# One 128x128 score product per chunk in a gated linear attention layer, with the prompt's keys scaled by 2^-16

## The chip, the cores and the metric

The kernel runs on one core of a Trainium2 chip. The metric is the device time of one execution in microseconds (us). TensorE is called PE in the profile (its weight loads PEld), VectorE DVE, ScalarE ACT, GpSimd POOL, and SyncE, which issues most of the transfers, SP.

## The reference

One decoder layer for 1024 prompt tokens and 32 sample tokens (8 sequences of 4), 1024 wide. An input projection feeds two groups: a recurrent group of 4 heads (HGRN2, a gated linear attention) and a convolution group with 31 taps. An output projection merges them. What matters here is the recurrent group:

```python
q = silu(q)
f = lb + (1 - lb) * sigmoid(fp);  k = 1 - f;  logf = log(f)
# per head, S is 128x128:  S_t = diag(f_t) S_{t-1} + k_t v_t^T ,  o_t = S_t^T q_t
o_a = rmsnorm(o_a, a_norm_g) * silu(za)
```

## The kernel before

**Projection.** `project` computes one block of 128 output channels for all 1056 tokens (1024 + 32). The inputs are split into a high and a low part (`wh`, `wl` of the weights; two tiles named `big` of the activations), and 3 x 24 matmuls of 128x352 run into three of four PSUM banks named `mm`. There are 24 such projections in the order `gb0 ga0 gb1 ga1 f0 q0 f1 q1 gb2 ga2 f2 q2 gb3 ga3 f3 q3`, then `za0..3` and `zb0..3`. The first part of the kernel, up to some 111 us, also makes the values `vt`; the output projection fills the time from some 390 us to the end.

**Heads.** Beside the projections two lists of generators are pumped: `hq` with the heads (`hgrn`) and `bg` with the convolution (`conv`), whose 30-odd taps per channel block are DVE instructions of about 512 elements. A head takes the prompt in two halves of 512 tokens, each of four chunks of 128 tokens; so there are 4 heads x 2 halves = 8 score blocks. In a half of the guarded fast path:

- `base` makes `qb` = q exp(g - m) and `kb` = k exp(m - g) on DVE and ACT, g being the running sum of log f in a chunk and m its value at token 63 (tiles `hw`);
- PE turns `kb` (`aux<-ident,hw`), ACT copies the result to `kT` (tile `ho`);
- PE makes the scores of each chunk in the bank `ptps` (`ptps<-hw`): 64 early keys against all 128 queries, and 64 late keys against the 64 late queries, the second with `tile_position=(0, 64)`. The quarter that neither writes was set to zero once by a memset;
- DVE copies the scores under a causal mask to `pt` (`COPY_PREDICATED`);
- PE makes the four chunks' state increments (`aux<-vt,ho`), DVE adds them up in `st`;
- PE adds `ops<-hw,st` (old state) and `ops<-pt,vt` (scores times values), and `head_norm` normalises over the head with ACT's Ln and Exp.

A 128x128 product in plain f32 (scores, state increments, outputs) leaves two MATMUL records in the trace; the projections' split products leave one each.

**The guard.** The fast path holds if the decay within half a chunk stays in a range (`RANGE`); a flag, computed in the kernel, starts a second, slower version (`emit` with `fast=False`) where it does not. That version is not executed here.

**What sets the order.** The program is written in the order of `project` and the pumps. A scheduler then orders the instructions of each engine by a simulated time with priorities, so a change of one instruction's length can move others. Each engine executes its own list in order.

Of the kernel before, what the change touches and what calls it, by code (L numbers as in the profile page):

```python
# [32 lines left out]
EPS = 1e-6  # L33
LB_MIN = 0.02
RANGE = 60.0
VPOS = 4
LEAD = 10.0
HU = 3
# [58 lines left out]
def emit(nc, tc, h, fast, flag_out=None):  # L97
    HW = 5
    with ExitStack() as ctx:
# [25 lines left out]
        make_identity(nc, ident)  # L125
        eps = sb([P, 1], "eps")
        nc.vector.memset(eps, EPS)
        avgr = sb([P, P], "avg", dt=F32R)
        avg = avgr.bitcast(F32)
        av = sb([P, P], "st", 5)  # L130
# [225 lines left out]

        lb = sb([P, 4], "lb")
        omlb = sb([P, 4], "omlb")
        nomlb = sb([P, 4], "nomlb")
        l0 = cols[:, C_LOG : C_LOG + 4]  # L360
        l1 = cols[:, C_LOG + 4 : C_LOG + 8]
        lt = sb([P, 12], "lt")
# [5 lines left out]
        V.reciprocal(lt[:, 0:4], lt[:, 0:4])  # L368
        V.tensor_tensor(lb, lt[:, 4:8], lt[:, 0:4], ALU.mult)
        V.tensor_scalar(omlb, lb, -1.0, 1.0, ALU.mult, ALU.add)  # L370
        V.tensor_scalar(nomlb, lb, -1.0, None, ALU.add)
        if fast:
            rng = sb([P, H, 16], "rng")
        wsum = sb([P, 60], "wsum")
# [87 lines left out]
        def hgrn(hd, q, k, g):  # L462
# [15 lines left out]
            for hf in range(2):  # L478
# [29 lines left out]
                    V.tensor_tensor(d3[:, :, r], d3[:, :, r], q3[:, :, r], ALU.mult)  # L508
                    return d

                def base(blk, idx, src=gv, n=512, mk=hw, qq=qv, kk=kv):
                    d = rel(blk, idx, src, n, mk)
                    kb = mk()
                    S.activation(kb, d, AF.Exp, scale=-1.0)
                    S.activation(d, d, AF.Exp)
                    V.tensor_tensor(kb, kb, kk, ALU.mult)
                    V.tensor_tensor(d, d, qq, ALU.mult)
                    return d, kb

# [3 lines left out]
                if fast:  # L523
# [8 lines left out]
                    S.copy(kT, kps)  # L532
                    for c in range(4):
                        cs = slice(c * P, (c + 1) * P)
                        c1, ce = c * P + P // 2, c * P + P

                        T.matmul(
                            ptps[0:64, cs], lhsT=kb[:, c * P : c1], rhs=qb[:, cs],
                            start=True, stop=True,
                        )  # L540
                        T.matmul(
                            ptps[64:P, c1:ce], lhsT=kb[:, c1:ce], rhs=qb[:, c1:ce],
                            start=True, stop=True, tile_position=(0, 64),
                        )
                    for pr in range(2):
                        masked(
                            pts[pr],
# [116 lines left out]
                        stop=True,  # L664
                    )
                yield
                yield from head_norm(hd, c0, 512, ops)
            if fast:
                end = sb([P, P], "st", 5)
                V.tensor_scalar(end, st, eg[:, 8:9], None, ALU.mult)  # L670
                st = end
            nc.sync.dma_start(h["o_hp"][hd], st)
            yield
# [4 lines left out]
            def sm():  # L678
# [6 lines left out]
            ki = rel(NS, NS - 1, gv, ST, sm)  # L685
            S.activation(ki, ki, AF.Exp, scale=-1.0)
            k4 = sb([P, 4, ST], "kts", 3)
            V.tensor_tensor(
                k4,
                ki.unsqueeze(1).to_broadcast([P, 4, ST]),  # L690
                kv.unsqueeze(1).to_broadcast([P, 4, ST]),
                ALU.mult,
            )
            kps = aux()
# [29 lines left out]
            yield  # L724
            sps = aux()
            if fast:
                qb, kb = base(NS, 1, gv, ST, sm, qv, kv)
                pairs = [(kb, qb)]
            else:
                pairs = []  # L730
                for hs in LEVELS[-2:]:
                    a = level(hs, gv, ST, sm, qv, kv)
                    pairs.append((a, a))
                pairs.append((kv, qv))
# [49 lines left out]
                    )  # L784
            nc.sync.dma_start(h["o_hs"][hd], so)
            yield
            yield from head_norm(hd, SEQ, ST, ops)
            hdone.add(hd)

        def head_norm(hd, c0, n, ops):  # L790
            lo = sb([P, 512], "ho", 2, F32R)
            hi = sb([P, 512], "ho", 2, F32R)
            r = late["mixa"][:, hd, c0 : c0 + n]
            S.activation(hi[:, 0:n], ops[:, 0:n], AF.Square)
            S.activation(r, ops[:, 0:n], AF.Square)
            V.tensor_tensor(lo[:, 0:n], r, hi[:, 0:n].bitcast(F32), ALU.subtract)
            ms = aux()
            mean(ms[:, 0:n], hi[:, 0:n], lo[:, 0:n])
            S.activation(r, ms[:, 0:n], AF.Ln, bias=eps)  # L799
            S.activation(r, r, AF.Exp, scale=-0.5)  # L800
            V.scalar_tensor_tensor(
                r, ops[:, 0:n], cols[:, C_HG : C_HG + 1], r, ALU.mult, ALU.mult
            )
            yield

# [161 lines left out]
        for i, (kind, c) in enumerate(order):  # L967
            if i == VPOS:
                t0 = T.ns
                for tb in range(2, 8):  # L970
                    v_block(tb)
                T.ns = t0
                ptps = bank("ptps", 1)
                V.memset(ptps, 0.0)
                late["ptps"] = ptps
                mixa = late["mixa"] = big()
            if i + 1 < len(order):
                ws.append(load_w(base_of[order[i + 1][0]] + order[i + 1][1]))
            w = ws.pop(0)
            nd = 1  # L980
            if kind == "gb":
                u = sb([P, 4 * MB], "u", 2)
                nc.gpsimd.memset(u[:, 0:PAD], 0.0)
                nc.sync.dma_start(
                    u[:, UW:UEND].rearrange("p (b t) -> p b t", t=PAD + NS)[:, :, 0:PAD], h["sc"][c]
                )
                cur["u"] = u
                project(
                    w, glu_evac(u, AF.Sigmoid, cols[:, C_BGLU + 4 + c : C_BGLU + 5 + c]), nd
                )  # L990
            elif kind == "ga":
                u = cur["u"]
                project(w, glu_evac(u, None, cols[:, C_BGLU + c : C_BGLU + c + 1]), nd)
                nc.sync.dma_start(h["o_cp"][c], u[:, SEQ:UW])
                nc.sync.dma_start(
                    h["o_cs"][c],
                    u[:, UW:UEND].rearrange("p (b t) -> p b t", t=PAD + NS)[:, :, NS:],
                )
                bg.append(conv(c, u))
                if c == 3:  # L1000
                    def lnp():
                        ln_pre()
                        yield

                    bg.insert(len(bg) - 1, lnp())
                    bg.append(ln_main())
            elif kind == "f":
                kt = sb([P, TOK], "qkg", 5)
                g = sb([P, TOK], "qkg", 5)
                project(w, act_into(kt, AF.Sigmoid), nd)  # L1010
                S.activation(g, kt, AF.Ln, bias=lb[:, c : c + 1], scale=omlb[:, c : c + 1])
                S.activation(
                    kt, kt, AF.Identity, bias=omlb[:, c : c + 1], scale=nomlb[:, c : c + 1]
                )
                for hf in range(4):
                    gs = g[:, hf * 256 : hf * 256 + 256]
                    V.tensor_tensor_scan(gs, rst, gs, 0.0, ALU.mult, ALU.add)
                gs = g[:, SEQ:TOK]
                V.tensor_tensor_scan(gs, rsts, gs, 0.0, ALU.mult, ALU.add)
                cur["kt"], cur["g"] = kt, g  # L1020
            elif kind == "q":
                q = sb([P, TOK], "qkg", 5)
                project(w, act_into(q, AF.Silu), nd)
                hq.append(hgrn(c, q, cur["kt"], cur["g"]))
            elif kind == "za":
                z = silu_tile()
                project(w, act_into(z, AF.Silu), nd)
                while c not in hdone:
                    step(hq)
                V.tensor_tensor(mixa[:, c, :], mixa[:, c, :], z, ALU.mult)  # L1030
            else:
                z = silu_tile()
                zb.append(z)
                if c == 2:
                    while not ln_state["done"]:
                        step(bg)
                    n0 = len(ln_state["done"])
                    project(
                        w,
                        act_into(z, AF.Silu),  # L1040
                        nd,
                        more=[partial(ln_silu, j, nb) for nb in range(n0) for j in range(4)],
                    )
                    for nb in range(n0):
                        ln_gate(nb, range(3))
                elif c == 3:
                    drain(1000)
                    project(
                        w,
                        act_into(z, AF.Silu),  # L1050
                        0,
                        (0, 1, 2),
                        more=[partial(ln_silu, j, nb) for nb in range(n0, 3) for j in range(4)],
                    )
                    for nb in range(3):
                        ln_gate(nb, range(3, 4) if nb < n0 else range(4))
                else:
                    project(w, act_into(z, AF.Silu), nd)
            if kind == "ga" and c == 0:
                V.ns = T.ns  # L1060
# [295 lines left out]
```

## Time and profile before

| | |
|---|---|
| median of 3 runs | 500.35 us (499.99 to 501.29) |
| the profiled execution | 500.03 us, its span 498.2 us |
| busy PE, DVE, ACT | 484.2, 358.6, 250.6 us |
| granted TensorE clock | 0.993 |
| DMA | 43.52 MB, mean 87 GB/s |

The page lists busy time by engine, the span in 40 slices, the chain of work that ended last and the costliest groups of instructions. In a timeline a row reads: start, duration, engine, line, operation, output<-inputs, shape, count, and in brackets the idle time of the engine before it with what ended it. PE's matmuls are pipelined, so the records overlap; what a piece of work costs PE is the time from start to start. `L72` is the line of a helper that records every DVE and PE operation, so the tile names tell the instructions apart.

### The profile page before, as it was taken

Reading aid. Unit: us, or ns where it says so; the run is one execution under the profiler, and the core shown is the slowest. Engines: PE = TensorE matmul, PEld = TensorE weight load, DVE = VectorE, ACT = ScalarE, POOL = GpSimd, SP = SyncE. Lnnn points to the kernel's source line nnn. Section 1 sums busy time; section 2 is a strip of 40 time slices with the busy share of each in tenths; the row PEclk is TensorE's granted clock in tenths of the full one; section 3 lists DMA queues with packets and bytes.
Section 4 is the critical chain, followed back from the end, with each engine's and each line's share of the span. In section 5 each row is a group of like instructions: output and inputs, shape, how many; then the busy total and the mean of one; then the engine's idle time right before and its main releaser. Section 6 shows DMA issues by size and latency. Waiting matters only on the chain.

```text
span 498.2 us, 7600 instructions
## 1 busy us (share of the span) xinstructions
PE 484.2 (97%) x3020; PEld 442.7 (89%) x3020; DVE 358.6 (72%) x682; ACT 250.6 (50%) x439; POOL 3.0 (1%) x20
## 2 busy tenths in 40 slices
PE   6999999999999999999999999999999999999992
PEld 5788899999999998999999999999999977877781
DVE  4864213999999989998999988993677747543441
ACT  5764332413646554635536554545766985422321
POOL 1000000000000000000000000000000000000000
PEclk9999999999999999999999999999999999999997
DMA  7910501231111213211123101131115396432111
GB/s 272 314 43 13 170 25 30 42 62 36 42 44 43 52 49 61 88 43 43 48 55 128 27 27 49 42 128 44 47 43 180 89 415 202 153 114 86 42 53 49
DMA packets 23003, 43.52 MB, mean 87 GB/s; under 512 B 10640, under 2 KB 11920, under 8 KB 22960
## 3 DMA queue, kind: packets, MB, share of 16 engines
q1 hardware_dynamic: 21808, 40.86, 26.3%
q10 hardware_dynamic: 1152, 2.10, 1.1%
q8 instruction: 25, 0.41, 0.3%
q14 instruction: 18, 0.15, 0.1%
HBM read 35.72 MB, written 7.24 MB: 86 GB/s over the span
## 4 chain that ended last, share of the span: by engine, by line
PE 90%; ACT 4%; DMA 3%; DVE 2%; issue 1%; SPq 0%; DVEq 0%
PE mm L72 70%; PE ops L72 8%; PE ptps L72 6%; PE aux L72 5%; DMA u<-gin 1%; ACT big L954 1%; DMA raw<-wo 1%; DMA o_hs<-raw 1%; DVE raw L72 1%; ACT L455 1%; DVE qkg L72 0%; ACT big L1100 0%; DVE big L72 0%; ACT qkg L455 0%; DVE u L72 0%
## 5 line engine op out<-in xcount | busy, mean ns | idle before, releaser
L72 PE MATMUL mm<-big,wh 128*128 128x352 f32 (+1 forms) x1280 | 323.7, 332 | 0.0
L72 PEld LDWEIGHTS mm<-big,wh 128*128 128x128 f32 x1280 | 224.1, 188 | 8.1 <-issue 1.6
L72 PE MATMUL mm<-big,wl 128*128 128x352 f32 (+1 forms) x640 | 211.4, 331 | 0.0
L72 PEld LDWEIGHTS mm<-big,wl 128*128 128x128 f32 x640 | 120.5, 188 | 3.4 <-issue 0.4
L72 DVE TENSOR_TENSOR wl<-wraw,wh 128x1024 fp32r<-128x1024 f32 x24 | 29.3, 1222 | 25.9 <-ACT wh L390 25.8
L72 DVE SCALAR_TENSOR_TENSOR big<-u,wsum,big 128x511 f32<-128x511 f32 (+14 forms) x60 | 44.5, 741 | 0.6
L72 DVE SCALAR_TENSOR_TENSOR big<-u,cols,big 128x511 f32<-128x511 f32 (+14 forms) x60 | 44.0, 735 | 0.0
L72 DVE SCALAR_TENSOR_TENSOR cq<-u,cols,cq 128x511 f32<-128x511 f32 (+13 forms) x56 | 41.2, 735 | 0.0
L72 DVE TENSOR_TENSOR qkg<-mm,big 128x512 f32<-128x512 f32 x16 | 10.9, 690 | 35.7 <-PE mm L72 35.7
L390 ACT CAST wh<-wraw 128x1024 fp32r<-128x1024 f32 x24 | 25.1, 1047 | 17.2 <-issue 7.8
L72 PE MATMUL mm<-vt,wh 128*128 128x512 f32 x64 | 25.6, 402 | 0.4 <-ACT wh L1167 0.4
L395 ACT ACT_TABLE_LOAD x20 | 25.7, 1283 | 0.3
L455 ACT ACTIVATE qkg<-mm 128x352 f32<-128x352 f32 x48 | 19.4, 465 | 11.4 <-PE mm L72 11.3
L72 PE MATMUL mm<-vt,wl 128*128 128x512 f32 x64 | 24.8, 390 | 0.0
L1204 ACT ACTIVATE big<-qkg 128x512 f32<-128x512 f32 x16 | 10.0, 628 | 29.1 <-DVE qkg L72 29.1
L455 ACT ACT_TABLE_LOAD x16 | 20.5, 1283 | 1.3 <-PE mm L72 1.0
L72 PE MATMUL ops<-big 128*128 128x512 f32 x64 | 20.8, 403 | 0.2 <-ACT big L197 0.2
L72 PE MATMUL ptps<-big 128*128 128x512 f32 x64 | 19.9, 394 | 0.0
L1167 ACT CAST wh<-big 128x512 fp32r<-128x512 f32 x16 | 9.2, 617 | 19.1 <-PE mm L72 18.6
L72 PEld LDWEIGHTS mm<-vt,wh 128*128 128x128 f32 x64 | 12.0, 188 | 5.2 <-ACT wh L1167 1.7
L72 PE MATMUL mm<-hw,wh 128*128 128x512 f32 x40 | 15.7, 392 | 0.0
L799 ACT ACTIVATE big<-aux,eps 128x512 f32<-128x512 f32 (+1 forms) x12 | 6.7, 556 | 17.9 <-PE aux L72 17.5
(239 smaller groups left out, 634.7 us busy)
## 6 DMA issues: line engine op xcount, KB each, us to landing
wraw<-win SPq DMA_DIRECT2D x24, 512.0 KB, 3.6
wraw<-wo SPq DMA_DIRECT2D x12, 512.0 KB, 3.7
big<-xp SPq DMA_DIRECT2D x2, 2048.0 KB, 10.1
big<-xp SPq DMA_DIRECT2D x4, 512.0 KB, 10.7
raw<-sh SPq DMA_DIRECT2D x4, 512.0 KB, 3.5
o_hs<-raw SPq DMA_DIRECT2D x4, 512.0 KB, 3.0
raw<-wo SPq DMA_DIRECT2D x4, 512.0 KB, 5.2
o_yp<-qkg ACTq DMA_DIRECT2D x8, 256.0 KB, 2.9
```

Of the source, the lines that this page charges most:

```text
L72: return f(*a, **k)
L390: S.copy(hi, wr)
L395: after(S.preload_act_table_set("natural_log_exp_and_others"), prev)
L455: return [S.activation(dst[:, nb * MB : (nb + 1) * MB], ps, func, bias=bias)]
L799: S.activation(r, ms[:, 0:n], AF.Ln, bias=eps)
L954: return S.activation(cv[:, c, cs], cv[:, c, cs], AF.Silu, bias=cols[:, C_LNB + c : C_LNB + c + 1], scale=cols[:, C_LNG + c : C_LNG + c + 1],)
L1167: S.copy(hv, m[:, :, ts])
L1204: S.activation(xr[:, hs], y[:, hs], AF.Square, accum_out=sqs[:, half : half + 1])
```

## The change

The two products of a chunk become one product of 128 keys by 128 queries, which fills the whole bank, and the memset of the bank goes. The late keys against the early queries, which the mask drops, are now computed too; so that they stay finite the keys are scaled by `KS` = 2^-16: the ACT instruction that makes k from the sigmoid takes its factors from `kb0` and `kw` (in place of `omlb` and `nomlb`). The factor is taken out again in the head's norm (`scale` of the Ln, and `hgk` in place of the gain), at the end in the final state (a second factor in the `TENSOR_SCALAR`), and for the sample tokens in two products, which become `SCALAR_TENSOR_TENSOR`.

```diff
-        nomlb = sb([P, 4], "nomlb")
+        kc = sb([P, 9], "kc")
+        kb0, kw, hgk = kc[:, 0:4], kc[:, 4:8], kc[:, 8:9]
...
-        V.tensor_scalar(nomlb, lb, -1.0, None, ALU.add)
+        V.tensor_scalar(kb0, lb, -ks, ks, ALU.mult, ALU.add)
+        V.tensor_scalar(kw, lb, ks, -ks, ALU.mult, ALU.add)
+        V.tensor_scalar(hgk, cols[:, C_HG : C_HG + 1], 1.0 / ks, None, ALU.mult)
...
                     S.activation(kb, d, AF.Exp, scale=-1.0)
                     S.activation(d, d, AF.Exp)
-                    V.tensor_tensor(kb, kb, kk, ALU.mult)
+                    if ks == 1.0:
+                        V.tensor_tensor(kb, kb, kk, ALU.mult)
+                    else:
+                        V.scalar_tensor_tensor(kb, kb, 1.0 / ks, kk, ALU.mult, ALU.mult)
...
                     for c in range(4):
                         cs = slice(c * P, (c + 1) * P)
-                        c1, ce = c * P + P // 2, c * P + P
-                        T.matmul(
-                            ptps[0:64, cs], lhsT=kb[:, c * P : c1], rhs=qb[:, cs],
-                            start=True, stop=True,
-                        )
-                        T.matmul(
-                            ptps[64:P, c1:ce], lhsT=kb[:, c1:ce], rhs=qb[:, c1:ce],
-                            start=True, stop=True, tile_position=(0, 64),
-                        )
+                        T.matmul(ptps[:, cs], lhsT=kb[:, cs], rhs=qb[:, cs], start=True, stop=True)
...
-                V.tensor_scalar(end, st, eg[:, 8:9], None, ALU.mult)
+                V.tensor_scalar(end, st, eg[:, 8:9], 1.0 / ks, ALU.mult, ALU.mult)
...
-            S.activation(r, ms[:, 0:n], AF.Ln, bias=eps)
+            S.activation(r, ms[:, 0:n], AF.Ln, bias=eps, scale=1.0 / (ks * ks))
...
                 ptps = bank("ptps", 1)
-                V.memset(ptps, 0.0)
```

The line numbers shift by one to three. The scheduler's order changes as well; three places follow.

PE, second half of head 1 (around 207 us in the trace of before). Before, the score products are broken up by the state increments and one output product:

```order
L72 MATMUL mm<-big,wl 128x352
L72 MATMUL ptps<-hw 64x128
L72 MATMUL ptps<-hw 64x64
L72 MATMUL ptps<-hw 64x128
L72 MATMUL aux<-vt,ho 128x128 x4
L72 MATMUL ptps<-hw 64x64
L72 MATMUL ops<-pt_421,vt 128x128
L72 MATMUL ptps<-hw 64x128
L72 MATMUL ptps<-hw 64x64
L72 MATMUL ptps<-hw 64x128
L72 MATMUL ptps<-hw 64x64
```

The same place in the changed kernel:

```order
L73 MATMUL mm<-big,wh 128x352
L73 MATMUL ptps<-hw 128x128 x4
L73 MATMUL mm<-big,wh 128x352
L73 MATMUL mm<-big,wl 128x352
L73 MATMUL mm<-big,wh 128x352 x2
L73 MATMUL mm<-big,wl 128x352
L73 MATMUL mm<-big,wh 128x352 x2
L73 MATMUL mm<-big,wl 128x352
L73 MATMUL mm<-big,wh 128x352 x2
L73 MATMUL aux<-vt,ho 128x128 x4
```

The four products now stand together, and the state increments come ten projection matmuls later. Counted in projection matmuls, the block's first score stands at 825 of 1728; before it stood at 803.

PE, second half of head 3 (around 333 us), before:

```order
L72 MATMUL mm<-big,wh 128x352 x2
L72 MATMUL ptps<-hw 64x128
L72 MATMUL aux<-vt,ho 128x128 x4
L72 MATMUL ptps<-hw 64x64
L72 MATMUL ptps<-hw 64x128
L72 MATMUL ptps<-hw 64x64
L72 MATMUL ptps<-hw 64x128
L72 MATMUL ptps<-hw 64x64
L72 MATMUL ptps<-hw 64x128
L72 MATMUL ptps<-hw 64x64
L72 MATMUL ops<-pt_421,vt 128x128
L72 MATMUL mm<-big,wl 128x352
```

and in the changed kernel:

```order
L73 MATMUL mm<-big,wh 128x352
L73 MATMUL ptps<-hw 128x128
L73 MATMUL aux<-vt,ho 128x128 x4
L73 MATMUL ptps<-hw 128x128 x2
L73 MATMUL ops<-pt_421,vt 128x128
L73 MATMUL ptps<-hw 128x128
L73 MATMUL mm<-big,wh 128x352
```

Here the block stays broken up, but all products in it now have one shape. From projection matmul 1546 on PE's list has the same instructions at the same places as before.

DVE, first half of head 0 (around 149 us): the first state copy `st<-aux`, which waits for the state increments, before:

```order
L72 SCALAR_TENSOR_TENSOR big<-u,cols,big 128x497
L72 COPY st<-aux 128x128
L72 TENSOR_TENSOR wl<-wraw,wh 128x1024
L72 SCALAR_TENSOR_TENSOR big<-u,wsum,big 128x501
L72 TENSOR_TENSOR hw<-hw,qkg 128x512
L72 SCALAR_TENSOR_TENSOR cq<-u,cols,cq 128x500
L72 SCALAR_TENSOR_TENSOR qkg<-rst,qkg 128x256 x4
L72 SCALAR_TENSOR_TENSOR qkg<-rsts,qkg 128x32
```

and in the changed kernel:

```order
L73 SCALAR_TENSOR_TENSOR cq<-u,cols,cq 128x500
L73 SCALAR_TENSOR_TENSOR qkg<-rst,qkg 128x256 x4
L73 SCALAR_TENSOR_TENSOR qkg<-rsts,qkg 128x32
L73 TENSOR_TENSOR hw<-hw,qkg 128x512
L73 TENSOR_TENSOR u<-u 128x512
L73 TENSOR_TENSOR hw<-hw,qkg 128x512
L73 SCALAR_TENSOR_TENSOR big<-u,wsum,big 128x500
L73 COPY st<-aux 128x128
L73 SCALAR_TENSOR_TENSOR cq<-u,cols,cq 128x499
```

The copy (and with it the state increments on PE, now at projection matmul 541 instead of 515) comes after the scans (`qkg<-rst,qkg`) and after the next half's products.

More of the change, by code (lines that the diff above doesn't have):

```diff
@@ L35 @@
 RANGE = 60.0
+KS = 2.0 ** -16
 VPOS = 4
@@ L127, in emit @@
         nc.vector.memset(eps, EPS)
+        ks = KS if fast else 1.0
         avgr = sb([P, P], "avg", dt=F32R)
@@ L509, in level, with base @@
                     return d
-                def base(blk, idx, src=gv, n=512, mk=hw, qq=qv, kk=kv):
+                def base(blk, idx, src=gv, n=512, mk=hw, qq=qv, kk=kv, ks=1.0):
                     d = rel(blk, idx, src, n, mk)
@@ L666, in hgrn @@
                 yield
-                yield from head_norm(hd, c0, 512, ops)
+                yield from head_norm(hd, c0, 512, ops, ks, hgk)
             if fast:
                 end = sb([P, P], "st", 5)
-                V.tensor_scalar(end, st, eg[:, 8:9], None, ALU.mult)
+                V.tensor_scalar(end, st, eg[:, 8:9], 1.0 / ks, ALU.mult, ALU.mult)
                 st = end
@@ L687, in hgrn @@
             k4 = sb([P, 4, ST], "kts", 3)
-            V.tensor_tensor(
+            V.scalar_tensor_tensor(
                 k4,
                 ki.unsqueeze(1).to_broadcast([P, 4, ST]),
+                1.0 / ks,
                 kv.unsqueeze(1).to_broadcast([P, 4, ST]),
+                ALU.mult,
                 ALU.mult,
@@ L726, in hgrn @@
             if fast:
-                qb, kb = base(NS, 1, gv, ST, sm, qv, kv)
+                qb, kb = base(NS, 1, gv, ST, sm, qv, kv, ks)
                 pairs = [(kb, qb)]
@@ L786, in hgrn, with head_norm @@
             yield
-            yield from head_norm(hd, SEQ, ST, ops)
+            yield from head_norm(hd, SEQ, ST, ops, 1.0, cols[:, C_HG : C_HG + 1])
             hdone.add(hd)
-        def head_norm(hd, c0, n, ops):
+        def head_norm(hd, c0, n, ops, ks, hg):
             lo = sb([P, 512], "ho", 2, F32R)
@@ L798, in head_norm @@
             mean(ms[:, 0:n], hi[:, 0:n], lo[:, 0:n])
-            S.activation(r, ms[:, 0:n], AF.Ln, bias=eps)
+            S.activation(r, ms[:, 0:n], AF.Ln, bias=eps, scale=1.0 / (ks * ks))
             S.activation(r, r, AF.Exp, scale=-0.5)
             V.scalar_tensor_tensor(
-                r, ops[:, 0:n], cols[:, C_HG : C_HG + 1], r, ALU.mult, ALU.mult
+                r, ops[:, 0:n], hg, r, ALU.mult, ALU.mult
             )
@@ L1012, in emit @@
                 S.activation(
-                    kt, kt, AF.Identity, bias=omlb[:, c : c + 1], scale=nomlb[:, c : c + 1]
+                    kt, kt, AF.Identity, bias=kb0[:, c : c + 1], scale=kw[:, c : c + 1]
                 )
```

## Prediction, made before the run

> **What bounds the kernel now.** I read the page's busy times first, then busy time by stage, then the waits of PE, then timelines of PE around the score blocks, and last the chain of waits at the place where PE does wait.
>
> ```profile
> PE 484.2 (97%) x3020; PEld 442.7 (89%) x3020; DVE 358.6 (72%) x682; ACT 250.6 (50%) x439; POOL 3.0 (1%) x20
> ```
>
> PE is busy for 97% of the span. Busy shares of PE flatter, since pipelined records overlap; the stage table says where the share is earned and what DVE, the runner-up, does meanwhile (columns: stretch, its length, then busy time and count of PE, PEld, DVE, ACT, POOL, the granted clock, DMA).
>
> ```profile
> core 0: us, PE busy (x) PEld busy (x) DVE busy (x) ACT busy (x) POOL busy (x), PEclk, DMA share, GB/s
> 145.00:345.00 200.00, 200.00 (x1389) 191.32 (x1388) 181.61 (x358) 107.41 (x176) 0.25 (x2) 1.00 0.20 58
> ```
>
> In these 200 us lie all score blocks but their consumers' tail. PE has no idle time, at full clock; DVE has 18.4 us of it. The list of waits of PE is empty from 14 to 401 us. So PE's own list sets the time, and time taken out of it comes off the end, as long as no wait takes its place.
>
> **The score block, the main term.** The timeline around the first block (first half of head 0):
>
> ```profile
> 146.50 0.32 PE L72 MATMUL mm<-big,wl 128*128 128x352 f32 x1
> 146.75 0.85 PEld L72 LDWEIGHTS ptps<-hw 128*64 128x64 f32 x16 [0.21 <-issue]
> 146.75 1.09 PE L72 MATMUL ptps<-hw 128*64 128x128 f32 x16
> 147.77 0.30 PEld L72 LDWEIGHTS mm<-big,wh 128*128 128x128 f32 x2 [0.17 <-issue]
> 147.77 0.59 PE L72 MATMUL mm<-big,wh 128*128 128x352 f32 x2
> 148.20 0.32 PE L72 MATMUL mm<-big,wl 128*128 128x352 f32 x1
> 148.30 0.73 DVE L72 SCALAR_TENSOR_TENSOR big<-u,wsum,big 128x502 f32<-128x502 f32 x1
> 148.36 0.48 PE L72 MATMUL mm<-big,wh 128*128 128x352 f32 x2
> 148.68 0.32 PE L72 MATMUL mm<-big,wl 128*128 128x352 f32 x1
> 148.84 1.05 PE L72 MATMUL aux<-vt,ho 128*128 128x128 f32 x8
> 149.65 0.57 PE L72 MATMUL mm<-big,wh 128*128 128x352 f32 x2
> 150.05 0.32 PE L72 MATMUL mm<-big,wl 128*128 128x352 f32 x1
> ```
>
> Undisturbed, a 352-column matmul starts 0.16 us after the last (148.20 to 148.36). From 146.50 to 148.20 PE issues three of these and the 16 records of a score block: 1.70 - 3 x 0.16 = 1.22 us for the block. From 148.68 to 150.05 it issues three and the 8 records of the state increments: 1.37 - 0.48 = 0.89 us. The state increments are four plain f32 products of 128x128 by 128x128, just what the score block becomes, so I take 0.89 us as the new price. The gain is 0.33 us a block. The weight loader's idle time says where it lies: 0.21 us before the first 64-column load and 0.17 us after the last, while the first state increment starts 0.16 us after the matmul ahead of it, as if nothing had changed. Half the records go, but that alone gains little: 16 records take 1.02 us from 146.75 to 147.77, 64 ns each, and 8 take 0.81 us from 148.84 to 149.65, 101 ns each, so two products of 64 columns mostly overlap.
>
> On that the Trainium skill has two rules. "TensorE: Matmul & The Clock Gate", Part 3, "Measured speedup vs the span model", has products on different column tiles run together, a pack costing one product and some 4 ns for each further tile; by this rule alone eight packs cost little more than eight full records, about 8 x 4 ns a block, and the whole change would give an estimated 0.3 us. "TensorEngine Tiling", "Key Properties", says that a change of tiling mode drains the array; the two idle times around the block agree with that, and a run without the 64-column tiles is what will show it.
>
> **The two broken blocks.** In two of the eight blocks the scheduler had put full-width products between the 64-column ones. Second half of head 1, then second half of head 3:
>
> ```profile
> 207.36 0.32 PE L72 MATMUL mm<-big,wl 128*128 128x352 f32 x1
> 207.61 0.65 PE L72 MATMUL ptps<-hw 128*64 128x128 f32 x6
> 208.19 1.16 PE L72 MATMUL aux<-vt,ho 128*128 128x128 f32 x8
> 209.28 0.33 PE L72 MATMUL ptps<-hw 128*64 128x64 f32 x2
> 209.54 0.49 PE L72 MATMUL ops<-pt,vt 128*128 128x128 f32 x2
> 209.96 0.65 PE L72 MATMUL ptps<-hw 128*64 128x128 f32 x8
> 210.54 0.59 PE L72 MATMUL mm<-big,wh 128*128 128x352 f32 x2
> 210.97 0.32 PE L72 MATMUL mm<-big,wl 128*128 128x352 f32 x1
> ```
>
> ```profile
> 332.58 0.48 PE L72 MATMUL mm<-big,wh 128*128 128x352 f32 x2
> 333.00 0.43 PE L72 MATMUL ptps<-hw 128*64 128x128 f32 x2
> 333.36 1.16 PE L72 MATMUL aux<-vt,ho 128*128 128x128 f32 x8
> 334.45 0.88 PE L72 MATMUL ptps<-hw 128*64 128x64 f32 x14
> 335.25 0.49 PE L72 MATMUL ops<-pt,vt 128*128 128x128 f32 x2
> 335.50 0.41 PE L72 MATMUL mm<-big,wl 128*128 128x352 f32 x1
> 335.74 0.32 PE L72 MATMUL mm<-big,wh 128*128 128x352 f32 x1
> ```
>
> The first stretch takes 210.97 - 207.36 - 3 x 0.16 = 3.13 us, the second 335.74 - 332.74 - 2 x 0.16 = 2.68 us (332.74 is the start of the second matmul of its first row). Each holds a score block, a block of state increments and one output product. At the undisturbed price that is 0.89 + 0.89 + 0.22 = 2.00 us (a product is a quarter of 0.89). They give back 1.13 and 0.68 us. In the new order the first of them is whole, the second is still broken, but by products of the same width: no switch is left to pay.
>
> **Sum on PE:** 6 x 0.33 = 1.98, plus 1.13, plus 0.68: 3.8 us. Bounds: if only the smaller of the two visible idle times goes, 8 x 0.17 = 1.4 us; if a full-width block also loses the 0.08 us that the state increments still pay on their way out (149.65 to 150.05 is 0.40 us for two matmuls), 3.8 + 8 x 0.08 = 4.4 us. A dearer block is excluded by the row of the state increments, the same instruction by shape and type, and for that reason I take 3.8.
>
> **What else the change does.** All of this is off PE:
>
> ```profile
> 113.05 0.48 DVE L72 MEMSET ptps<- 128x512 f32 x1
> L72 DVE SCALAR_TENSOR_TENSOR st<-st,eg,aux 128x128 f32<-128x128 f32 x28 | 9.7, 345 | 1.3 <-PE aux L72 1.1
> L72 DVE TENSOR_TENSOR kts<-sm,qkg x4: 272/286/293, 140.7 to 319.3; 128x128 f32<-128x128 f32 x4
> L72 DVE TENSOR_SCALAR nomlb<-lb x1: 164/164/164, 26.7 to 26.7; 128x4 f32<-128x4 f32 x1
> ```
>
> The memset (0.48 us of DVE) goes. The sample keys' product becomes a SCALAR_TENSOR_TENSOR: 345 against 286 ns at 128x128, 4 x 0.06 = 0.24 us of DVE, and the 32-column one of each head rises by no more than that. Two more tiny setup instructions cost 2 x 0.16 us at 27 us. Together at most +0.3 us of DVE, covered by its 18.4 us of slack under PE; were that cover gone, 0.3 us is the price. The new scales on ACT's Ln and Identity and the second factor of the final state stay within instructions that run anyway: no added instruction, hence nothing. No transfer is added. On SP two stores of states (`o_hp`, `o_hs`) each go behind one weight load more:
>
> ```profile
> wraw<-win SPq DMA_DIRECT2D x24, 512.0 KB, 3.6
> ```
>
> Such a load lands in 3.6 us; the store behind it frees a buffer (`raw`) for the next head's sample state, whose products come once a head, (319.3 - 140.7) / 3 = 60 us apart by the `kts` row, which covers a delay of that size; PE reads nothing of it before.
>
> **What is moved.** On PE the blocks come later by up to some 30 projection matmuls, on DVE the first state copy comes after the scans. Each hand-off from DVE to PE could now be late. The first one, before:
>
> ```profile
> 141.64 0.69 DVE L72 TENSOR_TENSOR hw<-hw,qkg 128x512 f32<-128x512 f32 x1
> ```
>
> The second operand of the block at 146.75 was ready at 142.33, 4.4 us early. PE moves ahead by some 0.3 us from one block to the next, and the scheduler has moved the blocks back in its list, so the margin is not used up by the gain itself; how much of it the new order of DVE uses is not told by the trace.
>
> **The end.** At 402 us PE has one wait, for the last link of a chain through four other engines and queues:
>
> ```profile
> 373.73 1.90 DVE raw L72 x7
> 375.65 3.27 DMA o_hs<-raw
> 378.94 4.00 DMA raw<-wo
> 402.61 0.50 PE L72 MATMUL mm<-vt,wh 128*128 128x512 f32 x1 [0.41 <-ACT wh L1167]
> ```
>
> Had that chain a start of its own, the gain would end here as a longer wait. But it hangs on PE: head 3's sample states (`raw`) follow the last sample product, then their store, then the load of an output weight into the same buffer, then ACT's casts and silus. PE's list is unchanged over this stretch, so the chain starts 3.8 us earlier with PE. The 0.41 us wait stays as it is.
>
> So the profiled execution, 500.03 us with a span of 498.2, becomes 500.03 - 3.8 = 496.2 us; it stood 0.3 us under the median of its runs, so the forecast is **496.5 us** against 500.35.
>
> **Rivals.**
> *Part of it comes back as waits.* DVE is 91% busy from 145 to 345 us and its list is reordered. A hand-off that falls behind one more convolution tap waits up to 0.73 us (148.30). One to three such on PE leave 3.8 - 0.7 to 3.8 - 2.2, that is 1.6 to 3.1 us: 497.2 to 498.8. For it: the second state copy's shift; against it: PE has no such wait at any hand-off now. Chance 0.16.
> *The gain never reaches the end.* Either the chain at 402 us does not move with PE, so that 0.41 us of waiting becomes 4.2 us, and the time is 500.35; or the idle times of 0.21 and 0.17 us belong to the score operands and not to the width, a full-width block keeps them, and only the records that do not overlap are saved, 1.02 - 0.81 - 0.17 = 0.04 us a block or 0.3 us in all: 500.0 us. Against the first speaks that the chain's first link waits for PE; against the second, that the broken blocks cost more at each change of width. Chance 0.10. The span model named above leads to the second of these.
> *Slower.* One mechanism: the new order puts a projection's matmuls behind outputs (`ops<-hw,st`) whose state DVE makes too late, since the state copy now stands behind scans and the next half's products. PE's list is strictly in order, so everything waits. It decides from 5.3 us of such waits on (3.8 gained plus 1.5 lost), seven taps' worth; twelve outputs late by one tap each give 12 x 0.73 = 8.8 us of waits: 500.35 - 3.8 + 8.8 = 505.3 us. Against it: PE's outputs have been moved later as well. Chance 0.04.
>
> **How the numbers follow.** Within 0.3% (1.5 us) a measurement of this kernel tells nothing from no change. The forecast has 0.70 (495.9 to 497.2, the sum's upper bound of 4.4 us and half a microsecond of wait as its own range), the partial gain 0.16, both faster by over 0.3% but for the partial one's last 0.1 us: faster 0.86. The gain lost is "same", 0.10; slower 0.04. The range for 8 in 10 reaches from 495.4, half a microsecond of the runs' spread (499.99 to 501.29) under the upper bound, to 498.8, the end of the partial gain.
>
> **What the profile after would show.** The score group with 128x128 weights and 64 records; a block costing 0.89 us from start to start, and no idle time of the weight loader ahead of it; stretches of 2.0 us in place of 3.13 and 2.68; PE's waits still empty from 14 to about 397 us; the wait at the output projection still about 0.4 us, at about 398.8. Wrong would be the forecast if PE's list of waits shows DVE between 145 and 345 us, if the last wait grows by microseconds, or if the new block costs more than the state increments.

## The result: 0.65% faster, and the profile after

The changed kernel took 497.62 us against 500.69 us for the kernel before, timed in the same rounds: a ratio of 0.9935, 95% interval 0.9917 to 0.9953. Timed again in another job it took 497.15 us (496.69 to 498.62) against 501.16: 0.9925, 0.9910 to 0.9939. By these ratios the change is worth 3.25 and 3.75 us. Single executions of 1225.88 us (the changed kernel), 2285.23 and 689.65 us (the kernel before) are left out of the ratios, though not of the medians. The forecast, 496.5 us, is a ratio of 0.9923 and lies in both intervals.

The page of the changed kernel, busy time by engine, and the row of the stage that the prediction rested on (columns as before):

```profile
PE 482.2 (97%) x2956; PEld 444.0 (89%) x2956; DVE 358.1 (72%) x683; ACT 251.0 (51%) x439; POOL 2.9 (1%) x20
```

```profile
145.00:345.00 200.00, 200.00 (x1349) 195.07 (x1348) 182.10 (x360) 106.54 (x175) 0.25 (x2) 1.00 0.21 58
```

64 records fewer on PE, which is still busy throughout these 200 us. The weight loader's busy time rose here from 191.32 to 195.07 us in the same stretch: its idle time fell from 8.7 to 4.9 us. DVE's busy time hardly moved. The score group, all records of one shape now, and the first block on PE and on the weight loader, in timelines of the changed kernel:

```profile
L73 PE MATMUL ptps<-hw x64: 270/275/276, 148.4 to 335.5; 128*128 128x128 f32 x64
```

```profile
148.22 0.33 PE L73 MATMUL mm<-big,wh 128*128 128x352 f32 x1
148.39 1.05 PE L73 MATMUL ptps<-hw 128*128 128x128 f32 x8
149.20 0.40 PE L73 MATMUL mm<-big,wh 128*128 128x352 f32 x1
149.44 0.32 PE L73 MATMUL mm<-big,wl 128*128 128x352 f32 x1
```

```profile
148.23 1.02 PEld L73 LDWEIGHTS ptps<-hw 128*128 128x128 f32 x8
```

From 148.22 to 149.44 PE issues two projection matmuls and the block: 1.22 - 2 x 0.16 = 0.90 us, where 0.89 was expected and 1.22 stood before. The loader has no idle time in brackets ahead of the block, and the first score starts 0.17 us after the matmul before it (148.22 to 148.39), as any other matmul would.

Single records tell where the 0.32 us lay. The last record of the block, before and after:

```profile
147.57 0.27 PE L72 MATMUL ptps<-hw 128*64 128x128 f32 x1
```

```profile
149.17 0.28 PE L73 MATMUL ptps<-hw 128*128 128x128 f32 x1
```

On the way in, the first score started 0.25 us after the matmul before it (146.50 to 146.75) and now starts 0.17 us after it. From the first record to the last the narrow block took 0.82 us (146.75 to 147.57), the full one takes 0.78 (148.39 to 149.17). From the last record to the next projection matmul it was 0.20 us (147.57 to 147.77) and is 0.03 (149.17 to 149.20), and from that matmul to the one behind it 0.27 us (148.20 - 147.77 - 0.16) and now 0.24. So half as many records gain only some 0.04 us a block, the figure that the prediction's second rival gives them; the other 0.28 us lie where the width changes. The narrow records did not queue one behind the other: in the trace the eight of the early keys start 0.11 us apart but for the first, and those of the late keys, on the other 64-column tile, start among them.

The stretch in head 3 that stayed broken up:

```profile
333.39 0.32 PE L73 MATMUL mm<-big,wh 128*128 128x352 f32 x1
333.55 0.39 PE L73 MATMUL ptps<-hw 128*128 128x128 f32 x2
333.78 1.06 PE L73 MATMUL aux<-vt,ho 128*128 128x128 f32 x8
334.67 0.61 PE L73 MATMUL ptps<-hw 128*128 128x128 f32 x4
335.12 0.39 PE L73 MATMUL ops<-pt,vt 128*128 128x128 f32 x2
335.34 0.39 PE L73 MATMUL ptps<-hw 128*128 128x128 f32 x2
335.48 0.41 PE L73 MATMUL mm<-big,wh 128*128 128x352 f32 x1
335.73 0.32 PE L73 MATMUL mm<-big,wl 128*128 128x352 f32 x1
```

It takes 335.73 - 333.39 - 2 x 0.16 = 2.02 us (2.00 expected, 2.68 before). It is as broken as ever; only the changes of width are gone.

**How much PE's list became shorter.** Both kernels issue the same 1728 matmuls of the projections, so their starts can be compared number by number. The first stands at 57.35 us before and at 58.91 after, 1.56 us *later*; this difference stays the same up to the first score block. Number 1584, behind the last block, stands at 369.31 before and at 366.89 after, 2.42 us earlier. The stages between gave 1.56 + 2.42 = 3.98 us; the prediction's sum was 3.8. The profile of the second job shows the same: 1.28 later, then 2.70 earlier, 3.98 us.

**The 1.56 us at the start** are a stretch of low clock. The changed kernel by windows (the column after the POOL count is the granted clock):

```profile
12.00:14.00 2.00, 1.54 (x8) 1.10 (x9) 2.00 (x2) 0.59 (x2) 0.00 (x0) 0.90 1.00 393
14.00:16.00 2.00, 2.00 (x8) 1.71 (x7) 1.56 (x3) 1.73 (x3) 0.12 (x1) 0.50 1.07 274
16.00:18.00 2.00, 2.00 (x8) 1.54 (x8) 1.75 (x3) 2.00 (x3) 0.00 (x0) 0.75 1.01 395
```

In the kernel before, the same windows show 1.00. The clock missing in the three windows, (0.10 + 0.50 + 0.25) x 2 us = 1.7 us, about covers the delay. The delay is a matter of the single execution rather than of the scaling: over the kernels below, their profiles have the first projection matmul 0.02, 0.10, 0.67, 0.67, 0.80, 0.83, 1.28 and 1.55 us later than the profile of before, and the smallest belongs to a kernel with all the scaling edits. The profile of before and the two with 0.02 and 0.10 us have no such stretch; each of the seven others has one of 3.4 us at half clock within its first 17 us. "TensorE: Matmul & The Clock Gate" of the Trainium skill, Part 1, "What's actually happening", says that the gate counts activity in a free-running window, so that the slow stretch at a kernel's start varies from run to run, and is below 1% of a typical span. The traces agree that it varies, and 1.56 of 496.4 us is 0.3%; but here the clock was full from 8 to 12 us, so the stretch came behind PE's first matmuls and not at them.

**The end.** PE's list of waits from 55 to 420 us, and links of the chain of waits, in the changed kernel:

```profile
PE mm L73 <- ACT wh L1169: 0.4, 1, 0.4
PE mm L73 <- ACT qkg L461: 0.2, 1, 0.2
```

```profile
371.86 1.90 DVE raw L73 x7
...
373.78 3.24 DMA o_hs<-raw
...
377.04 3.88 DMA raw<-wo
```

The wait at the output projection stayed (0.38 us, at 400.2). A new one of 0.2 us came at 385 us; in the profile of the second job it is 0.8 us. The chain's links start 1.87, 1.87 and 1.90 us earlier than before (`raw`, its store, the load into it), while PE's number 1584 starts 2.42 us earlier. What stands on DVE's list just ahead of the additions into `raw` is the same in both kernels, here before and after:

```profile
372.21 1.23 DVE L72 TENSOR_TENSOR wl<-wraw,wh 128x1024 fp32r<-128x1024 f32 x1 [2.19 <-ACT wh L390]
```

```profile
370.34 1.23 DVE L73 TENSOR_TENSOR wl<-wraw,wh 128x1024 fp32r<-128x1024 f32 x1 [2.18 <-ACT wh L396]
```

It waits for ACT's cast `wh`, it moved by the same 1.87 us, and the additions start 0.03 us after its end. At the last projection matmul (1727) PE's lead is down from 2.42 to 2.03 us: 0.39 us given back between 367 and 393 us. At PE's last instruction it is 1.80.

### The profile page after: what moved, and what is told of

Read it like the earlier page. It is cut to its first block, busy times and chain, and to the rows that moved or that the text cites. A ratio compares the mean times of both kernels' runs of the same rounds, so it can differ in the third digit from the quotient of the medians.

```text
span 496.4 us, 7472 instructions
## 1 busy us (share of the span) xinstructions
PE 482.2 (97%) x2956; PEld 444.0 (89%) x2956; DVE 358.1 (72%) x683; ACT 251.0 (51%) x439; POOL 2.9 (1%) x20
## 4 chain that ended last, share of the span: by engine, by line
PE 87%; ACT 5%; DVE 4%; DMA 3%; issue 1%; SPq 0%; DVEq 0%; ACTq 0%
PE mm L73 67%; PE ops L73 8%; PE ptps L73 6%; PE aux L73 5%; DVE big L73 1%; DMA u<-gin 1%; ACT big L957 1%; DMA raw<-wo 1%; ACT L461 1%; DMA o_hs<-raw 1%; DVE raw L73 1%; DVE u L73 1%; DVE hw L73 1%; DVE qkg L73 0%; ACT big L1102 0%
## 5 line engine op out<-in xcount | busy, mean ns | idle before, releaser
L883 ACT ACTIVATE u<-mm,cols 128x352 f32<-128x352 f32 (+2 forms) x16 | 6.5, 484 | 18.1 <-PE mm L73 18.0
```

The lines of the kernel that those rows point to most:

```text
L883: out.append(S.activation(dst, src, func, bias=bias))
```

## Experiments

Three explanations of the gain were open. The prediction's: a change of tile width between 64 and 128 columns drains PE, and the change removes all of them. Its first rival: fewer records, each with a price of its own. Its second: not the products at all, but the memset, the new order or the scaling. All experiments start from the changed kernel; the diffs are against it.

**The changed kernel again** (no edit).

> The changed kernel once more, unaltered, for a narrower interval and a second profile. If the granted clock's dip at 14 to 17 us in the first profile (1.56 us late at the first projection) was chance, the profile here has no such lead and its span is 3.4 to 4.0 us under before's. The ratio to before is 0.992 to 0.995 by the theory of the switch of tiling mode (3.8 us less PE work, some 0.4 us of it given back at the end); above 0.997 the gain was luck.

Measured: 497.15 us against 501.16, ratio 0.9925 [0.9910, 0.9939], that is 3.75 us by the ratio; PE's list gave 3.98 us up to number 1584 once more, and lost 1.04 us of lead from there to number 1727. What PE earns repeats to the hundredth; what is given back does not. The stretch of low clock at the start, expected to be gone if it was chance, came again (1.28 us); that it belongs to the execution rests on the other profiles named above.

**The scaling without the wide product.** Two products of 64 columns and the memset again, all other edits of the change kept.

```diff
-  T.matmul(ptps[:, cs], lhsT=kb[:, cs], rhs=qb[:, cs], start=True, stop=True)
+  T.matmul(ptps[0:64, cs], lhsT=kb[:, c * P : c1], rhs=qb[:, cs], start=True, stop=True)
+  T.matmul(ptps[64:P, c1:ce], lhsT=kb[:, c1:ce], rhs=qb[:, c1:ce],
+           start=True, stop=True, tile_position=(0, 64))
...
   ptps = bank("ptps", 1)
+  V.memset(ptps, 0.0)
```

> All of the scaling is kept, but the score products are again two per chunk, 64 keys each, and the memset is back. Theory S (the switch between 64-column and 128-column tiles costs PE time): the whole gain is gone, ratio to before 0.999 to 1.002, a whole score block costs 1.22 us again. Rival O (the gain comes from the scheduler's new order and from the scaling's other edits): part of it stays, ratio 0.996 or less.

Measured: 500.86 us against 501.16, ratio 1.000 [0.9989, 1.001]. Its first block in the timeline of PE:

```profile
146.53 0.32 PE L73 MATMUL mm<-big,wl 128*128 128x352 f32 x1
146.77 1.09 PE L73 MATMUL ptps<-hw 128*64 128x128 f32 x16
147.79 0.59 PE L73 MATMUL mm<-big,wh 128*128 128x352 f32 x2
148.22 0.32 PE L73 MATMUL mm<-big,wl 128*128 128x352 f32 x1
```

148.22 - 146.53 - 3 x 0.16 = 1.21 us: the price of before. The scaling, its norm and its state edits cost nothing that can be measured, as the prediction put it, and they gain nothing. The whole gain hangs on the product's shape (with the order that follows from it).

**Twice the records, all of full width.** Each product of 128 keys by 128 queries as two of 128 keys by 64 queries: 16 records a block as before the change, but no 64-column weights.

```diff
-  T.matmul(ptps[:, cs], lhsT=kb[:, cs], rhs=qb[:, cs], start=True, stop=True)
+  for q0 in (0, 64):
+      qs = slice(c * P + q0, c * P + q0 + 64)
+      T.matmul(ptps[:, qs], lhsT=kb[:, cs], rhs=qb[:, qs], start=True, stop=True)
```

> As the changed kernel, but each chunk's score is two products over 64 queries each, all 128 keys as weights: as many products as before the change, none of them on a 64-column tile. Theory S: no idle time of the weight loader around the block, whatever the block costs inside. Rival R (what was saved is the number of records, or an idle time that any score block has because of its operands): idle time of some 0.2 us before and after it as before the change. The block's own cost tells the price of a record: 16 x 0.11 = 1.8 us if a record of 128 weight columns costs 0.11 us however few columns it streams (about 7 us slower than the changed kernel), 0.9 us if the streamed columns set it (no difference).

Measured: 509.88 us (508.96 to 510.81), ratio 1.0181 [1.0153, 1.021], from two executions. The first block:

```profile
148.21 0.33 PE L73 MATMUL mm<-big,wh 128*128 128x352 f32 x1
148.38 1.89 PE L73 MATMUL ptps<-hw 128*128 128x64 f32 x16
150.08 0.41 PE L73 MATMUL mm<-big,wh 128*128 128x352 f32 x1
150.32 0.32 PE L73 MATMUL mm<-big,wl 128*128 128x352 f32 x1
```

150.32 - 148.21 - 0.32 = 1.79 us, twice the 0.90 of the changed kernel, although the same number of columns is streamed. The loader goes through the block without a pause in front of it:

```profile
148.21 1.92 PEld L73 LDWEIGHTS ptps<-hw 128*128 128x128 f32 x16
```

A record of 128-column weights costs 0.106 us (1.70 us over 16) whether 64 or 128 columns pass. So at full width the number of records sets the price. With 64-column weights it did not, since the records of the two tiles ran side by side: 16 of them took as long as eight full ones, apart from the changes of width. And the idle times of 0.21 and 0.17 us do not come with the operands of a score block, as this block has the same operands and no idle time.

The total is some 5 us dearer than eight blocks explain (8 x 0.89 = 7.1 of 12.7 us). The rest appears late, at the output projection:

```profile
413.38 0.79 PE L73 MATMUL mm<-vt,wh 128*128 128x512 f32 x1 [2.88 <-ACT wh L1173]
413.97 0.63 PE L73 MATMUL mm<-hw,wh 128*128 128x512 f32 x1
414.39 0.63 PE L73 MATMUL mm<-vt,wh 128*128 128x512 f32 x1
...
419.09 0.84 PE L73 MATMUL mm<-vt,wl 128*128 128x512 f32 x2
```

The wait that is 0.38 us in the changed kernel is 2.88 us here, and behind it a 512-column matmul takes 0.43 us from start to start where 0.23 is normal (420.00 to 420.23 in the same trace):

```profile
415.00:420.00 5.00, 5.00 (x14) 3.84 (x13) 1.22 (x1) 0.19 (x1) 0.00 (x0) 0.55 0.75 254
```

The granted clock is down to 0.55. From 413.97 to 419.09 stand 12 such steps, some 12 x 0.2 = 2.4 us lost. With 2.5 us of added wait that makes 4.9 us. That the order which the scheduler found for this kernel made the cast late is how the chain reads; it was not tried separately.

**A probe of each width.** One extra product of 32 columns streamed ahead of each score block, once with 64 and once, as the control, with 128 keys. Its result is overwritten by the first score product.

```diff
+  T.matmul(ptps[0:64, 0:32], lhsT=kb[:, 0:64], rhs=qb[:, 0:32], start=True, stop=True)   # first
+  T.matmul(ptps[:, 0:32], lhsT=kb[:, 0:P], rhs=qb[:, 0:32], start=True, stop=True)       # control
   for c in range(4):
```

> As the changed kernel, plus one small product ahead of each score block on a 64-column tile (64 keys, 32 queries, two records), whose result the block then overwrites. Theory S: entering and leaving the narrow tile costs PE time whatever runs on it, so a block with its probe costs 0.89 + 0.2 to 0.45 us and the weight loader shows idle time (0.1 to 0.2 us) at the two changes of width. Rival R (width does not matter, records and their weight columns do): two records of 64 weight columns cost at most what half of two full ones cost, 0.11 us, less than the control with 128 columns.

> The control: the same small product with all 128 keys as weights, so on the full array. Theory S: two more records of 0.11 us, block with probe 0.89 + 0.22 = 1.11 us, no idle time of the weight loader; less than with the narrow probe. Rival R: more than with the narrow probe.

Measured, one execution each, so that the totals say little: 499.69 us with the narrow probe, 498.26 us with the wide one. The first block with the narrow probe, PE and weight loader, and then the same with the wide one (a row with x10 joins the two records of the probe to the eight of the block):

```profile
147.33 0.32 PE L73 MATMUL mm<-big,wh 128*128 128x352 f32 x1
147.59 1.39 PE L73 MATMUL ptps<-hw 128*64 128x32 f32 x10
148.73 0.41 PE L73 MATMUL mm<-big,wh 128*128 128x352 f32 x1
148.97 0.32 PE L73 MATMUL mm<-big,wl 128*128 128x352 f32 x1
```

```profile
147.58 1.20 PEld L73 LDWEIGHTS ptps<-hw 128*64 128x64 f32 x10 [0.22 <-DVE big L73]
```

```profile
146.76 0.33 PE L73 MATMUL mm<-big,wh 128*128 128x352 f32 x1
146.92 1.28 PE L73 MATMUL ptps<-hw 128*128 128x32 f32 x10
147.95 0.41 PE L73 MATMUL mm<-big,wh 128*128 128x352 f32 x1
148.20 0.33 PE L73 MATMUL mm<-big,wl 128*128 128x352 f32 x1
```

```profile
146.76 1.25 PEld L73 LDWEIGHTS ptps<-hw 128*128 128x128 f32 x10
```

Less two matmuls of 0.16 us, the narrow one takes 148.97 - 147.33 - 0.32 = 1.32 us, the wide one 148.20 - 146.76 - 0.32 = 1.12 us, the block alone 0.90. So a product with 128 keys adds 0.22 us, and one with half the keys adds 0.42 us. The loader's idle time of 0.22 us stands only in front of the narrow one. The releaser that the row names, DVE's `big`, is no explanation: all eight narrow probes have 0.22 us in front of them, put down to three different tiles of DVE or to `issue`, and the control has none in the same place. The second pause that was expected, on the way out, does not show in the loader (0.04 us). All eight blocks together say the same: up to number 1584, against the 3.98 us of the changed kernel, PE's list gains 0.70 us with the narrow probes and 2.40 us with the wide ones, so a probe costs 0.41 or 0.20 us. This is the direct sign of the switch: half the work, twice the price, in the same place in the list. The rule in "TensorEngine Tiling (Array Packing)", "Key Properties", of the Trainium skill, that a change of tiling mode drains TensorE, agrees; the price, 0.20 us above the control for one way in and out, comes from these rows.

**One half at a time.** The wide product in the second halves only (where the broken blocks were), then in the first halves only, with the memset back in both.

```diff
-  T.matmul(ptps[:, cs], lhsT=kb[:, cs], rhs=qb[:, cs], start=True, stop=True)
+  if hf == 1:     # first kernel; hf == 0 in the second
+      T.matmul(ptps[:, cs], lhsT=kb[:, cs], rhs=qb[:, cs], start=True, stop=True)
+  else:
+      ...         # the two 64-column products, as above
```

> The scaling everywhere; one product per chunk in the second half of each head, two as before the change in the first half. Both of the broken blocks of before are second halves. By the sum of the prediction 2 x 0.33 + 1.13 + 0.68 = 2.5 us of the 3.8 us come from here: ratio to before 0.9935 to 0.9965, blocks of 0.89 us in the second halves and of 1.22 us in the first. Rival O (the gain hangs on the order as a whole and does not split by blocks): anything from 0.992 to 1.000, without block costs that add up.

> The other four blocks: one product per chunk in the first half of each head, two in the second. By the prediction's sum 4 x 0.33 = 1.3 us, less what new breaks cost: the scheduler puts one output product between the narrow ones of head 0's second half too, some 0.3 us. Ratio 0.997 to 0.9985. Rival O as with the second halves; if both halves give about the same ratio, the price of broken blocks was wrong.

Measured: second halves 498.70 us against 500.63, ratio 0.9951 [0.9932, 0.9970], 2.5 us by the ratio; first halves 500.31 us, ratio 0.9995 [0.9983, 1.0007], 0.25 us with an interval of 0.6 to either side. The first was as expected. The second fell short, and its timeline shows where: in head 3 the remaining narrow products are broken up more than before (and in head 0 by output products, which the expectation had counted).

```profile
332.77 0.48 PE L73 MATMUL mm<-big,wh 128*128 128x352 f32 x2
333.18 0.43 PE L73 MATMUL ptps<-hw 128*64 128x128 f32 x2
333.54 1.16 PE L73 MATMUL aux<-vt,ho 128*128 128x128 f32 x8
334.63 0.45 PE L73 MATMUL ptps<-hw 128*64 128x64 f32 x6
335.01 0.49 PE L73 MATMUL ops<-pt,vt 128*128 128x128 f32 x2
335.43 0.65 PE L73 MATMUL ptps<-hw 128*64 128x128 f32 x8
336.01 0.43 PE L73 MATMUL mm<-big,wl 128*128 128x352 f32 x1
336.27 0.48 PE L73 MATMUL mm<-big,wh 128*128 128x352 f32 x2
```

336.27 - 332.93 - 2 x 0.16 = 3.02 us (332.93 is the start of the second matmul of the first row), against 2.68 in the kernel before: one stay at the narrow width was added and 0.34 us with it. PE's list gave 0.77 us up to number 1584 instead of 4 x 0.33 = 1.3. The two halves together, 2.45 + 0.25 = 2.7 us, stay under the 3.75 us of both at once, but with intervals of 1.0 and 0.6 us to either side this alone shows nothing. PE's list gave 2.83 and 0.77 us, 3.60 of the 3.98; the 0.38 us that are missing are about the size of the extra stay in head 3. The scheduler places the products anew for each kernel, and a placement between full-width products is free at one width (2.02 us above) and costs at two, so the parts need not add up.

**Without the wait at the end.** In the changed kernel the third and the sixth output weight share the buffer `raw` with head 3's sample states. Here only the sixth does; the third goes through `wraw`.

```diff
-  tag, bufs = ("raw", 1) if ko % 3 == 2 else ("wraw", 2)
+  tag, bufs = ("raw", 1) if ko == 5 else ("wraw", 2)
```

> As the changed kernel, but the third output weight is loaded into the buffers of the first two and the sixth into the buffer of the last head's sample states, so that the third does not wait for the store of those states. Theory T (the chain store, load, casts, silus is what PE waits for at the end, 0.4 us at the output projection and 0.2 us at a bank before it, and what ate 0.4 us of the gain): both waits go, 0.4 to 1.0 us faster than the changed kernel, ratio to before 0.991 to 0.993. Rival: the chain's later links (convolution norm, silus, gates) wait for other things as long, and the time stays within 0.3 us of the changed kernel.

Measured: 496.98 us (496.07 to 497.53), ratio 0.9924 [0.9907, 0.9940]. PE's list of waits between 55 and 420 us is empty in its profile: both end waits went with the shared buffer. From its first projection matmul to PE's last instruction it gains 4.13 us on the profile of before, against 3.36 and 2.69 us in the two profiles of the changed kernel. The medians do not separate it: 496.98 against 497.15 us, timed in the same rounds. The expected 0.4 to 1.0 us are not there; the rival's number came true, but not its reason, since both waits are gone. It has the lowest median of all kernels here, but that it beats the changed kernel is not shown.

## Why the prediction was right, and where it was off

- **What bounds the kernel.** Right. Time taken out of PE's list came off the end, all but 0.6 and 1.3 us in the two profiles.
- **The score block, 1.22 to 0.89 us.** Right: 0.90 us. The step from the state increments to the score block, same instruction by shape and type, held.
- **That the width is the cause.** Shown by three runs: the scaling with narrow products gives nothing (1.000), the narrow probe costs 0.42 against 0.22 us in the same place, and a block of 16 full-width records has no pause around it. The prediction's remark that fewer records gain little was right for this change: some 0.04 us a block, since the narrow records overlap. Its 64 ns for a narrow record are not a price of records, as they hold the 0.20 us behind the last one. At full width each record is paid for (0.106 us). The span model of the Trainium skill that the prediction weighed ("TensorE: Matmul & The Clock Gate", Part 3), by which narrow products share their time and the change would give 0.3 us, agrees with the inside of the block, 0.82 against 0.78 us; it has no term for the switch, and the measured 3.75 us decide against it as the price of the whole.
- **The broken blocks, 1.13 and 0.68 us.** Right in head 3, still broken: 2.02 us in place of 2.68. For head 1 no stretch of after holds the same work, so its 1.13 us stand only within the sum. The run with first halves shows the reverse: an extra stay at 64 columns in head 3 and 0.34 us more.
- **The sum, 3.8 us.** PE's list gave 3.98 us in both profiles of the changed kernel. The 0.18 us more stay within its upper bound of 4.4 us. Their place is not known.
- **DVE's edits at nothing.** Right: ratio 1.000 [0.9989, 1.001] with all of them in.
- **Hand-offs from DVE to PE.** Right: no wait of PE on DVE between 55 and 399 us. The rival with one to three waits behind a tap did not come.
- **The end, "the 0.41 us wait stays as it is".** The wait did (0.38 us). The step that failed is "the chain starts 3.8 us earlier with PE". The additions into `raw` do not start on PE's last sample product, which ends 0.6 us before them in the kernel before and 1.1 us before them in the changed one: in both kernels they start when DVE's `wl` ends, which waits for ACT's cast `wh`. These moved by 1.87 us where PE moved by 2.42. Why ACT's and DVE's lists moved by some 0.5 us less than PE's stays open. What came of it is a new wait for ACT's `qkg`, 0.2 and 0.8 us in two profiles, where PE's list of waits was forecast to be empty up to 397 us; it went with the shared buffer. Of the 3.98 us, 3.36 and 2.69 us arrive at PE's last instruction in these two profiles.
- **The time.** 496.5 us was forecast, 497.62 and 497.15 us were measured, with the kernel before at 500.69 and 501.16 in the same rounds (500.35 when the forecast was made). Between forecast and measurement lie 1.12 us in the first job and 0.65 in the second. The rise of the kernel before over 500.35 accounts for 0.34 us of the first and for all of the second; what is left is of the size of what was given back at the end. How the runs' spread divides between the start's clock and the end's waits stays open: a profile shows one execution, and the medians of the kernel with and without the waits lie 0.17 us apart.

## What to carry to other kernels

Where narrow matmul tiles stand in a stream of full-width ones, look at the weight loader's idle time before and after them, and at the start of the next full-width matmul: that is the price of the switch, 0.2 to 0.3 us for each stay at the narrow width here. Computing a quarter that a mask drops was cheaper than not computing it, as it made the width uniform. The scheduler here broke such groups up; so judge the change on the order it leads to, and expect that parts of it need not add up. One thing the runs do not cover: the guard allows an exponent of 60 in each half of a chunk, so a late key times an early query can reach e^120 / 2^16, more than f32 holds; inputs near that edge were not tried.

## What the runs showed of the hardware

- A narrow product of 64-column weights costs more than one of 128 in a full-width stream: 0.42 against 0.22 us.
- Sixteen records on two 64-column tiles overlap and take as long as eight full-width ones: 0.82 and 0.78 us from the first to the last start.
- A plain f32 record of 128-column weights costs some 0.1 us with 64 as with 128 columns streamed: 1.70 us for 16 and 0.81 us for 8 records.
- A wait of 2.88 us in front of the output projection was followed by some 6 us of granted clock near half (0.55 in the 5 us window), in which a 512-column matmul cost 0.43 in place of 0.23 us. The Trainium skill, "TensorE: Matmul & The Clock Gate", "HAM oscillation", puts the gap that drops the clock at about 3.4 us; in this run a shorter one was followed by the drop. The drop at 13.6 us in the changed kernel came after 6.8 us at full clock, in which no gap between PE's matmuls was longer than 1.2 us.
